# Prompt cross-attention scores: full float32 products replaced by three passes on split operands

## The chip, the core and the metric

The kernel runs on one NeuronCore of a Trainium2 chip. The metric is the device time of one execution in microseconds (us). The kernel before was timed in three runs: 813.55, 813.92 and 814.2 us, a median of 813.92 us. All times inside an execution come from one profiled execution of the same kernel.

## What is computed

The reference is one step of a decoder layer for two groups that share all weights: a prompt of 512 tokens and a sample group of 8 sequences of 4 tokens. A layer has a mixer (dilated attention and a gated recurrence), a cross-attention to a memory of 256 rows, and a feed-forward block. The change sits in the cross-attention, which reads in short:

```python
c = rmsnorm(x, norm_cross)
cq = (c @ w_cq).reshape(B, T, X_H, X_DH)                    # 4 heads of 128
s = jnp.einsum('bthd,bmhd->bhtm', cq, mem_k) * (X_DH ** -0.5)
pr = jax.nn.softmax(s, axis=-1)
co = jnp.einsum('bhtm,bmhd->bthd', pr, mem_v).reshape(B, T, X_W)
x = x + co @ w_co
```

For the prompt, mem_k and mem_v are projected from the memory inside the kernel; for the sample group they are read from a cache. All inputs and outputs are float32.

## The kernel before, in words

The activations lie transposed: 128 features on the partitions, the 512 prompt tokens and 32 sample tokens (544 columns) along the free axis. Every large projection is computed in two cuts of the columns, 0 to 255 and 256 to 543 (`CUTS`), and as three float32r passes: both operands are split into a high half (rounded to float32r, a copy on ACT) and a low half (the rest, a subtraction on DVE), and high x high, high x low and low x high are added up in PSUM. `split_half` (line 884) does such a split for an activation tile, `split_hi` and `split_lo` for a weight tile. Some small products are made with plain float32 operands instead; the prompt's scores against the memory are among them.

The memory's keys are written into two tiles `mk` (line 1707), two heads of 128 x 256 in each; the values into `mvt`, which are split into `mv_hl` (line 1863). The cross-attention then goes as follows.

- `dense_by_half` (line 856) computes cq. It runs the four heads' first cut, then calls `cq_after` (line 1896) for the four heads, then the four heads' second cut, and calls `cq_after` again. `cq_evac` scales the result out of PSUM into `cqT[h]` on DVE.
- `cross_prompt(h, part)` (line 1865) is called for each head and part. A part is 256 prompt tokens, two query blocks of 128. It makes the scores (two products of 128 x 128 by 128 x 256 into one PSUM bank, tile `ps_cp`), the row maxima (DVE, `cmx`), the exponentials (ACT, tile `cp`), the scaling by the reciprocal sum (one block on DVE, one on POOL), four transposes (`ps_cpt`), their split (`cpt..h`, `cpt..l`), the product with the split values (`ps_cpo`, three passes for each of the two blocks of memory rows), and the split of the result into `coh` and `col`. In the second part it also calls `cross_sample_scores` (line 1817), the sample group's scores (`ps_cs`), which use only 32 columns of the array at a time.
- `cross_sample` (line 1824) is the rest of the sample's cross-attention; its products with the cached values are `ps_cso`, and the values come in the tiles `st` from `in_mv`.
- `dense_by_half` (line 1914) then computes the output projection co, first cut of all eight blocks and then the second, from `coh` and `col`.

**What sets the order.** The instructions are not issued as written. The class `Tape` (line 251) records them as steps with an estimated length; `order` (line 435) plays a model of the five engines and picks the next step of each. Steps marked as main (the large projections) keep their order on PE. All other PE work is a side step: it is placed between main steps, in bursts, when enough of it has gathered, when it has waited long enough, or when its due time has come (line 573). Due times are worked out backwards from the users (`due`, line 397), and the estimated time of a main step is scaled by the sum of all PE lengths (`run`, line 421). A step may start only if the tiles that it writes are free. The working tiles of `A` and `R` (lines 668 and 671) come from one pool of 60 (`NA`, line 44); `leaves_room` (line 483) keeps a step from taking a tile that an earlier due step will want. PSUM has two banks for the main steps, five for side work (`PX`) and one for the sample group. Weights of w_cq and w_co are held in the same pool of 60 once they are split: four tiles for a column block of w_cq, two for one of w_co.

Of the kernel before, what the change touches and what calls it, by code (L numbers as in the profile page):

```python
# [10 lines left out]
F32 = mybir.dt.float32  # L11
F32R = mybir.dt.float32r
AF = mybir.ActivationFunctionType
ALU = mybir.AluOpType
# [640 lines left out]
def tile_decoder_step(ctx: ExitStack, tc: tile.TileContext, xT, memT, kwT, vw, s0, conv_in, mkT, mv, vecs, cst,  # L655
                      w_first, w_in, w_out, w_cq, w_ck, w_cv, w_co, w_gate, w_up, w_down,
                      yT, kT_out, vT_out, st_out, conv_out, mkT_out, mv_out, ss_out):
    nc = tape = Tape(tc.nc)
# [9 lines left out]
    def A(name, shape=None, dt=F32):  # L668
        return tape.tile(act, shape or [128, FW], dt, tag="a", name=name, bufs=NA)

    def R(name):
        return tape.tile(act, [128, FW], F32R, tag="a", name=name, bufs=NA)[:, :N]
# [4 lines left out]
    def PD(name):  # L677
        return tape.tile(psum, [128, 512], F32, tag="dense", name=name, bufs=2)

    def PX(name):  # L680
        return tape.tile(psum, [128, 512], F32, tag="aux", name=name, bufs=5)
# [26 lines left out]
    def C(name):  # L708
        lo, hi = CST_COLS[name]
        return cs[:, lo:hi] if hi <= mid else cs2[:, lo - mid:hi - mid]  # L710
# [173 lines left out]
    def split_half(src, name):  # L884
        n = src.shape[1]
        hi, lo = (R(f"{name}{p}")[:, :n] for p in "hl")
        nc.scalar.copy(hi, src)
        nc.vector.tensor_tensor(lo, src, hi.bitcast(F32), op=ALU.subtract)
        return hi, lo
# [71 lines left out]
    with tape.as_written():  # L961
# [42 lines left out]
        for n0, n in CUTS:  # L1004
            ps = PD(f"psr_mix_{n0}")
# [657 lines left out]
    for at, names in enumerate(MIX_ORDER):  # L1663
# [7 lines left out]
        else:  # L1671
            i = at - MIX_RAW
# [26 lines left out]
    ps = PX("psr_mem")  # L1699
# [7 lines left out]
    mk = [A(f"mk{i}", [128, 2, NMEM]) for i in range(2)]  # L1707
# [16 lines left out]
    for c in range(4):  # L1724
        ws.take()
        hi, lo = (t.rearrange("p k c -> p (k c)") for t in ws.whole[ws.i - 1][0][:2])
        for i in range(2):
            xh, xl = mems[2 * c + i]
            cols = slice(512 * i, 512 * i + 512)
            with tape.main():  # L1730
                for t in range(2):
                    tok = slice(128 * t, 128 * t + 128)
                    for j, (a, b) in enumerate(((xh, hi), (xl, hi), (xh, lo))):
                        nc.tensor.matmul(pcv[t], a[:, tok], b[:, cols], start=(c == 0 and i == 0 and j == 0),
                                         stop=(c == 3 and i == 1 and j == 2))
# [59 lines left out]
    def split_psum(h, ps, c0, c1):  # L1795
        hi, lo = (t[:, c0:c1] for t in co_hl[h])
        nc.scalar.copy(hi, ps)
        nc.vector.tensor_tensor(lo, ps, hi.bitcast(F32), op=ALU.subtract)

    def softmax_exp(ps, pt, name):  # L1800

        mx, den = small(f"cmx{name}", 2), small(f"cden{name}", 2)
        nc.vector.tensor_reduce(mx, ps.rearrange("p (a n) -> p a n", a=2), axis=AX.X, op=ALU.max, negate=True)
        for a in range(2):
            sl = slice(256 * a, 256 * a + 256)
            nc.scalar.activation(pt[:, sl], ps[:, sl], AF.Exp, bias=mx[:, a:a + 1], accum_out=den[:, a:a + 1])
        return den

    def softmax_scale(pt, den):
        nc.vector.reciprocal(den, den)  # L1810
        for a, eng in ((0, nc.vector), (1, nc.gpsimd)):
            sl = slice(256 * a, 256 * a + 256)
            eng.tensor_scalar(pt[:, sl], pt[:, sl], den[:, a:a + 1], None, op0=ALU.mult)
# [3 lines left out]
    def cross_sample_scores(h):  # L1817
        for g in range(2):
            kt = stream.take()
            for b in range(4):  # L1820
                nc.tensor.matmul(pss[32 * b:32 * b + 32, 256 * g:256 * g + 256], cqbd[:, 4 * g + b, h, :],
                                 kt[b], start=g == 0 and h == 0, stop=h == 3, skip_group_check=True)
# [38 lines left out]
            split_psum(h, pcs[:, 32 * h:32 * h + 32], SEQ, N)  # L1861

    mv_hl = [split_half(t[:, :512], f"mv{c}") for c, t in enumerate(mvt)]

    def cross_prompt(h, part):

        ps = PX(f"ps_cp{h}{part}")
        for a in range(2):
            qb = 2 * part + a
            nc.tensor.matmul(ps[:, 256 * a:256 * a + 256], cqT[h][:, 128 * qb:128 * qb + 128],  # L1870
                             mk[h // 2][:, h % 2, :], start=True, stop=True)
        if part:
            cross_sample_scores(h)
        pt = A(f"cp{h}{part}")
        den = softmax_exp(ps, pt, f"{h}{part}")
        softmax_scale(pt, den)
        pst = PX(f"ps_cpt{h}{part}")
        for c in range(2):
            for a in range(2):
                nc.tensor.transpose(pst[:, 256 * c + 128 * a:256 * c + 128 * a + 128],  # L1880
                                    pt[:, 256 * a + 128 * c:256 * a + 128 * c + 128], C("ident"))
        ptt = split_half(pst, f"cpt{h}{part}")
        po = PX(f"ps_cpo{h}{part}")
        for c in range(2):
            for i, (v, p) in enumerate(((0, 0), (0, 1), (1, 0))):
                nc.tensor.matmul(po[:, :256], mv_hl[c][v][:, 128 * h:128 * h + 128], ptt[p][:, 256 * c:256 * c + 256],
                                 start=c == 0 and i == 0, stop=c == 1 and i == 2)
        split_psum(h, po[:, :256], 256 * part, 256 * part + 256)

    cqT = [A(f"cq{h}") for h in range(XH)]  # L1890
# [5 lines left out]
    def cq_after(h, c):  # L1896
        if c:
            nc.gpsimd.tensor_copy(cqbd[:, :, h, 4 * h:4 * h + 4],
                                  cqT[h][:, SEQ:N].rearrange("p (b t) -> p b t", t=TS))
        cross_prompt(h, c)  # L1900
# [411 lines left out]
    for u, unit in enumerate(units + [None]):  # L2312
        per = next((each for halves, first, each in downs if first <= u and halves), (0, 0, 0, 0))
        q, b = unit.q if unit else {}, before.q if before else {}
# [72 lines left out]
    for m in range(KT):  # L2387
        t, hi, lo = (A(f"{n}z{m}", [128, k, 128], dt) for n, dt in (("wd", F32), ("wdh", F32R), ("wdl", F32R)))
# [89 lines left out]
```

## Time and profile before

| | |
|---|---|
| timed runs, median | 813.92 us |
| profiled execution, span from first to last instruction | 813.0 us |
| PE busy | 802.4 us, 99% of the span |
| DVE busy | 648.5 us, 80% |
| ACT busy | 445.0 us, 55% |
| POOL busy | 102.8 us, 13% |
| granted PE clock, mean | 0.998 |

The page gives no other time of the profiled execution than its span. PE stands for matmuls on TensorE, PEld for its weight loads, DVE, ACT and POOL for the vector, scalar and GpSimd engines; SPq marks the queue of SyncE, which issues most transfers. A line such as "PE ps_cp L650 x8" means eight recorded instructions that write the tile ps_cp; L650 is the recording helper of `Tape`, through which all instructions pass, so lines of code are told apart by tiles. A plain float32 matmul is recorded as two matmuls. Matmuls overlap, so the duration of one is longer than the distance to the next. In the timeline, square brackets hold the idle time of the engine before an instruction and what ended it.

### The profile page before, as it was taken

What the parts mean: (1) busy time and instruction counts of PE and PEld (TensorE: products, weight loads), DVE (VectorE), ACT (ScalarE), POOL (GpSimd) and SP (SyncE); (2) the same over time, 40 slices, a digit from 0 to 9 for tenths busy, and PEclk for the clock granted to TensorE, in tenths of its full rate; (3) what the DMA queues carried; (4) which work ended last, traced back from release to release, by engine and by line L of the source; (5) the groups of instructions that cost most, each with busy time, mean ns of one, the idle gap of its engine ahead of it and who ended that gap; (6) DMA issues with size and microseconds to landing.
All of it is one profiled execution on the core that took longest, in us unless ns stands there. A gap on an engine that the chain in (4) does not pass through costs nothing.

```text
span 813.0 us, 18994 instructions
## 1 busy us (share of the span) xinstructions
PE 802.4 (99%) x7531; PEld 755.4 (93%) x7531; DVE 648.5 (80%) x1458; ACT 445.0 (55%) x889; POOL 102.8 (13%) x186
## 2 busy tenths in 40 slices
PE   9999999999999999999999999999999999999996
PEld 9999986787889889999899999999999999999996
DVE  6996689966887897574689999997888788788854
ACT  7643365666657647454567655554554454445433
POOL 0021100010010000002201211211022012210013
PEclk9999999999999999999999999999999999999999
DMA  9449995955942454261734665655565555564503
GB/s 330 151 129 310 308 381 188 320 195 187 288 124 99 162 160 156 59 218 48 229 106 99 157 161 136 162 132 143 130 150 140 133 150 155 130 177 97 153 1 110
DMA packets 93065, 135.47 MB, mean 167 GB/s; under 512 B 6321, under 2 KB 60337, under 8 KB 92977
## 3 DMA queue, kind: packets, MB, share of 16 engines
q1 hardware_dynamic: 86208, 122.79, 46.8%
q0 software_dynamic: 5760, 10.49, 8.3%
q8 instruction: 59, 0.97, 0.5%
q10 hardware_dynamic: 1008, 0.99, 0.4%
q14 instruction: 30, 0.24, 0.1%
HBM read 126.17 MB, written 8.07 MB: 165 GB/s over the span
## 4 chain that ended last, share of the span: by engine, by line
PE 90%; DVE 5%; DMA 2%; ACT 2%; issue 1%; SPq 0%; DVEq 0%
PE ps_d L650 13%; PE ps_ag L650 7%; PE ps_au L650 7%; PE ps_wo L650 6%; PE ps_cu L650 4%; PE ps_cg L650 4%; PE ps_cq L650 3%; PE ps_dz L650 3%; PE ps_co L650 2%; PE ps_z_v L650 2%; PE ps_z_i L650 2%; PE ps_dg L650 2%; PE ps_du L650 2%; PE ps_z_Q L650 2%; PE ps_z_f L650 2%; PE ps_g L650 1%
## 5 line engine op out<-in xcount | busy, mean ns | idle before, releaser
L650 ACT CAST wh<-wr 128x1024 fp32r<-128x1024 f32 (+1 forms) x54 | 46.1, 873 | 45.3 <-PE ps_z_i L650 8.9
L650 DVE TENSOR_TENSOR wl<-wr,wh 128x1024 fp32r<-128x1024 f32 (+1 forms) x54 | 54.3, 1016 | 3.7 <-ACT wh L650 3.6
L650 DVE TENSOR_TENSOR xr<-xr,ps_d 128x256 f32<-128x256 f32 x80 | 34.6, 433 | 11.1 <-PE ps_d L650 10.2
L650 POOL COPY last<-ug 128x16 f32<-128x16 f32 (+1 forms) x44 | 22.6, 534 | 120.2 <-DVE ug L650 119.6
L650 DVE SCALAR_TENSOR_TENSOR cv<-ug,vec,cv 128x560 f32<-128x560 f32 x44 | 35.1, 798 | 2.5 <-ACT cv L650 1.9
L650 ACT ACTIVATE cv<-ug,vec 128x560 f32<-128x560 f32 x22 | 18.8, 856 | 15.5 <-DVE ug L650 15.4
L650 POOL TENSOR_TENSOR hvm<-hsm,cs 64x512 f32<-64x512 f32 x4 | 4.5, 1119 | 161.6 <-ACT hsm L650 161.6
L650 DVE TENSOR_TENSOR cv<-cv,r_ux 128x512 f32<-128x512 f32 (+1 forms) x44 | 18.7, 435 | 3.9 <-ACT cv L650 3.3
L650 ACT ACTIVATE P<-P,mx 128x128 f32<-128x128 f32 (+3 forms) x32 | 17.6, 553 | 6.7 <-DVE mx L650 6.7
L650 ACT ACTIVATE cv<-cv 128x560 f32<-128x560 f32 x22 | 14.8, 674 | 9.1 <-DVE cv L650 9.1
L624 POOL DMA_DIRECT2D S1u<-in_w_up x10 | 8.6, 863 | 87.4 <-DMA S1u<-in_w_up 27.6
L650 ACT COPY keptu<-ps_au 128x272 f32<-128x272 f32 x20 | 7.7, 386 | 21.1 <-PE ps_au L650 21.1
L650 ACT COPY keptg<-ps_ag 128x272 f32<-128x272 f32 x20 | 7.7, 385 | 21.0 <-PE ps_ag L650 20.7
L650 POOL TENSOR_SCALAR cp<-cp,cden 128x256 f32<-128x256 f32 x8 | 8.1, 1019 | 85.7 <-issue 76.2
L650 PE MATMUL ps_co<-coh,wh 128*128 128x256 f32 (+1 forms) x64 | 18.6, 291 | 0.0
L650 PE MATMUL ps_co<-coh,wl 128*128 128x256 f32 (+1 forms) x64 | 18.4, 288 | 0.0
L650 PE MATMUL ps_co<-col,wh 128*128 128x256 f32 (+1 forms) x64 | 18.4, 288 | 0.0
L650 DVE TENSOR_TENSOR xr<-xr,ps_wo 128x256 f32<-128x256 f32 (+1 forms) x16 | 6.8, 435 | 12.6 <-PE ps_wo L650 12.6
L650 DVE TENSOR_TENSOR xr<-xr,ps_dz 128x288 f32<-128x288 f32 (+1 forms) x15 | 6.6, 438 | 12.3 <-PE ps_dz L650 12.3
L650 PE MATMUL psdo<-st,dpt 128*32 128x256 f32 x224 | 16.2, 386 | 0.1
L650 ACT ACT_TABLE_LOAD x11 | 14.1, 1283 | 2.3 <-issue 2.1
L650 PE MATMUL psd<-st,qbd_win 128*32 128x224 f32 x256 | 15.4, 358 | 0.0
(3889 smaller groups left out, 3670.7 us busy)
## 6 DMA issues: line engine op xcount, KB each, us to landing
st<-in_kwT SPq DMA_DIRECT2D x32, 448.0 KB, 5.9
st<-in_vw SPq DMA_DIRECT2D x28, 512.0 KB, 5.7
wd<-in_w_down SPq DMA_DIRECT2D x32, 256.0 KB, 3.1
wr<-in_w_in SPq DMA_DIRECT2D x15, 512.0 KB, 6.6
wrg<-in_w_gate SPq DMA_DIRECT2D x10, 512.0 KB, 4.1
wru<-in_w_up SPq DMA_DIRECT2D x10, 512.0 KB, 4.5
st<-in_mkT SPq DMA_DIRECT2D x8, 512.0 KB, 6.8
wr<-in_w_out SPq DMA_DIRECT2D x8, 512.0 KB, 3.7
```

Of the source, the lines that this page charges most:

```text
L624: return tape.put(engine, lambda: call(*args, **kw), outs, ins, 0.1, 0.3, size)
L650: return tape.put(engine, lambda: call(*args, **kw), outs, ins, length, lag, size, port, words)
```

## The change

The keys of the memory are split once, right after the values: `mk_hl` holds a high and a low tile of 512 columns for each of the two `mk` tiles. In `cross_prompt`, a new tile `cqs` takes the high half of the part's 256 query columns (a copy on ACT) and the low half (a subtraction on DVE). Each of the two score products becomes three float32r products that add up in the same PSUM region: q high with mk high, q high with mk low, and q low with mk high; the product of the two low halves is left out, as in the kernel's other split products. Nothing else is edited; since the planner works from the recorded steps, the order of all instructions is made anew.

```diff
     mv_hl = [split_half(t[:, :512], f"mv{c}") for c, t in enumerate(mvt)]
+    mk_hl = [split_half(t.rearrange("p h n -> p (h n)"), f"mk{i}") for i, t in enumerate(mk)]
 
     def cross_prompt(h, part):
 
         ps = PX(f"ps_cp{h}{part}")
+        q = A(f"cqs{h}{part}", [128, 2, 256], F32R)
+        src, at = cqT[h][:, 256 * part:256 * part + 256], 256 * (h % 2)
+        nc.scalar.copy(q[:, 0, :], src)
+        nc.vector.tensor_tensor(q[:, 1, :], src, q[:, 0, :].bitcast(F32), op=ALU.subtract)
         for a in range(2):
-            qb = 2 * part + a
-            nc.tensor.matmul(ps[:, 256 * a:256 * a + 256], cqT[h][:, 128 * qb:128 * qb + 128],
-                             mk[h // 2][:, h % 2, :], start=True, stop=True)
+            for i, (n, m) in enumerate(((0, 0), (0, 1), (1, 0))):
+                nc.tensor.matmul(ps[:, 256 * a:256 * a + 256], q[:, n, 128 * a:128 * a + 128],
+                                 mk_hl[h // 2][m][:, at:at + 256], start=i == 0, stop=i == 2)
         if part:
             cross_sample_scores(h)
```

## The prediction

> **What bounds the kernel now.** I read the head of the page first (busy times and the chain by engine), then a table of stages, then the chain itself around the changed lines.
>
> ```profile
> span 813.0 us, 18994 instructions
> PE 802.4 (99%) x7531; PEld 755.4 (93%) x7531; DVE 648.5 (80%) x1458; ACT 445.0 (55%) x889; POOL 102.8 (13%) x186
> PE 90%; DVE 5%; DMA 2%; ACT 2%; issue 1%; SPq 0%; DVEq 0%
> ```
>
> PE is busy in 99% of the span, and 90% of the chain that ended last is PE work. The table of stages shows whether that also holds where the change sits (columns: stretch, length, then busy time and instruction count of PE, PEld, DVE, ACT, POOL; then the granted clock, DMA share, GB/s).
>
> ```profile
> 0.00:50.00 50.00, 48.27 (x362) 47.27 (x363) 42.67 (x84) 32.40 (x59) 3.64 (x10) 1.00 0.60 207
> 100.00:150.00 50.00, 48.53 (x768) 39.27 (x764) 46.20 (x138) 30.28 (x64) 2.11 (x3) 1.00 0.87 300
> 365.40:382.00 16.60, 16.60 (x124) 16.13 (x124) 7.40 (x18) 5.29 (x19) 4.19 (x5) 1.00 0.11 38
> 382.00:400.50 18.50, 18.50 (x166) 14.96 (x163) 10.63 (x23) 9.31 (x25) 2.01 (x4) 1.00 0.65 204
> 400.50:416.00 15.50, 15.41 (x166) 13.32 (x165) 13.13 (x33) 11.00 (x32) 4.10 (x5) 1.00 0.62 193
> 436.00:797.00 361.00, 361.00 (x2874) 360.95 (x2873) 301.59 (x609) 185.85 (x326) 65.25 (x128) 1.00 0.51 132
> ```
>
> From 365.4 to 400.5, where the prompt's scores are computed, PE is busy all the time at the full granted clock (1.00), while DVE and ACT are each busy for about half. From 436 to 797 PE never rests either, so a microsecond of PE time removed here should arrive at the end. The page gives the profiled execution only as its span, 813.0; the three timed runs have a median of 813.92, so about 0.9 us lies around the span, and I leave that as it is.
>
> **Step 1: the products.** Sixteen full float32 products (4 heads, 2 parts, 2 query blocks) go. Each is recorded as two matmuls, so the view of the tile ps_cp counts 32. In their place come 48 products of float32r operands, of the same 128 x 256 shape as the cq and cpo products. The chain gives whole groups of both kinds (start, length, what):
>
> ```profile
> L650 PE MATMUL ps_cp<-mk,cq x32: 377/379/483, 365.2 to 399.9; 128*128 128x256 f32 x32
> 362.57 2.82 PE ps_cq L650 x24
> 365.40 1.73 PE ps_cp L650 x8
> 373.03 1.73 PE ps_cp L650 x8
> 384.03 2.84 PE ps_cpo L650 x24
> 387.88 1.92 PE ps_cp L650 x8
> 397.18 1.08 PE ps_cp L650 x4
> ```
>
> The mean duration of one record (379 ns) can't be used, because matmuls overlap; the length of a group can. Eight ps_cp records, that is four products, take 1.73 us: 0.4325 us each. Twenty-four passes take 2.82 or 2.84 us: 0.118 us each, three of them 0.354. A product becomes 0.0787 us shorter, sixteen of them 1.26 us. This is the term that carries the forecast.
>
> [...]
>
> **Step 2: entering the products.** The visit at 387.88 took 0.19 us more than the 1.73 of the first two, and that at 397.18 took 1.08 for two products instead of 0.865, also 0.2 more. Both follow the sample's scores, which use 32 columns of the array. Is this price one of float32, which would go as well? A group of split passes behind narrow products elsewhere answers it:
>
> ```profile
> 57.26 1.65 PE psd L650 x32
> 58.91 1.70 PE ps_ck0k L650 x12
> 60.61 1.51 PE ps_ak0k L650 x12
> ```
>
> Twelve split passes take 1.70 us behind the narrow psd products and 1.51 otherwise, again 0.19. So the price belongs to the step from narrow to wide, and I take it as unchanged: 0. The bounds are three such visits without it (the third, at 399.17, stands below), a further gain of 0.6 us, and, if the new waits break the two pairs of visits that are now one group, two entries more, a loss of 0.4.
>
> **Step 3: the splits of mk and q.** ACT makes the high half, DVE the rest. The nearest rows are the same two operations on tiles of 128 x 256 and 128 x 512:
>
> ```profile
> L650 ACT CAST coh<-ps_cpo x8: 372/373/375, 384.8 to 415.5; 128x256 fp32r<-128x256 f32 x8
> L650 DVE TENSOR_TENSOR col<-ps_cpo,coh x8: 412/415/425, 386.0 to 416.2; 128x256 fp32r<-128x256 f32 x8
> L650 ACT CAST wh<-wr x19: 612/620/1054, 341.4 to 408.8; 128x512 fp32r<-128x512 f32 x16, 128x1024 fp32r<-128x1024 f32 x3
> L650 DVE TENSOR_TENSOR mk<-ps_ck,r_mem x4: 405/416/417, 277.8 to 291.6; 128x256 f32<-128x256 f32 x4
> L650 DVE TENSOR_TENSOR wl<-wr,wh x18: 672/683/1226, 342.4 to 410.7; 128x512 fp32r<-128x512 f32 x15, 128x1024 fp32r<-128x1024 f32 x3
> ```
>
> ACT gets 8 x 0.373 + 2 x 0.620 = 4.2 us, DVE 8 x 0.415 + 2 x 0.683 = 4.7 us. The mk part can run during the out projection, since mk is written by 292 us. The eight q splits fall between 364 and 400, where the table leaves ACT some 20 us free and DVE 17. As engine time they cost nothing; if their cover failed, what would show is their latency, the next step.
>
> **Step 4: the new waits.** Between the evacuation of cq (DVE) and the scores (PE) now stand a copy on ACT and a subtraction on DVE: 0.373 + 0.415 = 0.8 us and two handovers. PE takes its matmuls in the planned order, so behind a late split waits whatever was queued next on it, a half of cq or of co. On DVE the next evacuation of cq, which frees a PSUM bank, stands behind the subtraction, which waits for ACT. The timeline shows how close the two ends are (start, length, engine, what):
>
> ```profile
> 363.63 0.43 DVE L650 SCALAR_TENSOR_TENSOR cq<-ps_cq,r_cx 128x256 f32<-128x256 f32 x1 [1.32 <-ACT r_cx L650]
> 365.24 1.89 PE L650 MATMUL ps_cp<-mk,cq 128*128 128x256 f32 x8
> 396.22 0.46 DVE L650 SCALAR_TENSOR_TENSOR cq<-ps_cq,r_cx 128x288 f32<-128x288 f32 x1 [0.91 <-PE ps_cq L650]
> 399.17 1.13 PE L650 MATMUL ps_cp<-mk,cq 128*128 128x256 f32 x4
> 389.05 0.42 DVE L650 TENSOR_TENSOR col<-ps_cpo,coh 128x256 fp32r<-128x256 f32 x1 [1.44 <-PE ps_cp L650]
> L650 PE MATMUL ps_co<-coh,wh x12: 278/281/364, 400.5 to 405.1; 128*128 128x256 f32 x12
> 415.83 0.75 DVE L650 TENSOR_TENSOR col<-ps_cpo,coh 128x256 fp32r<-128x256 f32 x2
> 415.42 10.25 PE ps_co L650 x84
> ```
>
> Head 0 is ready at 364.06 and used at 365.24, 1.2 us later; head 3's second part at 396.68 and used at 399.17, 2.5 us later. Both hold the 0.8 us and the handovers. At the far end the last low half of co's input is written at 416.58. It is first needed when the first halves of co are through. Of their 96 passes 36 (three operand pairs of 12) run by 405.1, the other 60 head the group that starts at 415.42, at 0.118 each, hence until 422.5. So 5.9 us of cover remain at the end of this chain. I take 0; the bounds are 0 and 0.8 us on each of the four second-part visits, 3.2 us.
>
> **Step 5: tiles.** The pool of 60 working tiles matters, because the planner lets a step start only when its tile is free.
>
> ```profile
> 356.73 3.61 SPq L624 DMA_DIRECT2D st<-in_mv  x7
> 361.75 0.38 SPq L624 DMA_DIRECT2D st<-in_mv  x1
> 375.29 0.47 ACT L650 ACTIVATE cp<-ps_cp,cmx 128x256 f32<-128x256 f32 x1 [5.97 <-PE ps_cpt L650]
> 369.69 1.01 POOL L650 TENSOR_SCALAR cp<-cp,cden 128x256 f32<-128x256 f32 x1 [76.15 <-issue]
> 375.20 6.38 PE ps_cq L650 x48
> 389.80 6.38 PE ps_cq L650 x48
> 405.80 3.96 PE L650 MATMUL ps_cso<-st,cspt 128*32 128x256 f32 x64
> ```
>
> Around 377 us the code's tiles add up to 60: x 8, the split norm 16, w_cq 16, the eight half tiles of in_mv (all loaded by 362), mv 4, cq 4, mk 2, one row factor, one cp. The ACT row shows it: the second head's exponential waits 5.97 us, until the first head's transposes release a tile. The change holds mk as four tiles instead of two, and each q split takes one for a few microseconds, so about three more are wanted. What can yield without harm are the in_mv tiles, which are used only from 405.8 on. I take 0; what it costs otherwise is the third rival.
>
> The order of all instructions is planned anew from the changed costs. Where PE has no idle time that can move nothing; before 311 us the two stages with most of it lack 1.7 and 1.5 us, so I allow 0.3 us each way.
>
> Sum: 813.92 - 1.26 = 812.7, with 812.1 to 813.4 as this case's own range (below it the 0.6 us of step 2, above it the 0.4 of step 2 and 0.3 of replanning).
>
> **The rivals.**
> [...]
>
> Second, the gain is used up by waits: 0.3 us of uncovered handover at each of the four second-part visits, where PE waits for one head after another, gives back 1.2 us: 813.9. For it: on ACT and DVE other work stands ahead of the splits. Against it: the 2.5 us at the last head.
>
> Third, slower, by tiles: lacking a free tile, each of heads 1 to 3 has its softmax so late that its transposes miss one half of cq (6.38 / 2 = 3.19 us). The last low half of part 0 then moves by 9.6 us. It ended at 389.47, and cover lasts until the cq halves end at 396.18, 6.7 us later; PE idles 2.9 us and the net is 813.92 - 1.26 + 2.9 = 815.6. Four halves give 818.7. I take 816. It decides from 6.7 us of delay on. For it speaks the 5.97 us row; against it the in_mv tiles, and that a cq half frees four weight tiles.
>
> **How the numbers follow.** Forecast 0.56, first rival 0.15, second 0.16, third 0.13. A measurement of this kernel can tell about 0.2%, 1.63 us: faster means below 812.29, slower above 815.55. Faster: most of the first rival (0.13) and a quarter of the forecast (0.14), 0.27. Slower: the third rival, 0.13. The same: 0.60. The range goes from 811.7 (the first rival less 0.3 of replanning) to 815.6, which cuts most of the third rival.
>
> **What would show it.** In the profile after: 48 ps_cp matmuls, 24 of them in 2.8 us or 12 in 1.4; PE's busy time lower by 1.3; PE still at its whole length in 365 to 400; first co passes 1 us or so earlier. Wrong would be PE idle with cqs, cp or coh as releaser, a w_co or in_mv load that ends a wait of PE, or groups of ps_cp passes above 0.13 us each.

## The result, and the profile after

The changed kernel took 816.26 us (median of 22 runs, 814.94 to 818.98); the kernel before, run in turn with it, 814.61 us (22 runs, 813.55 to 816.74). The ratio is 1.0021, with a 95% interval of 1.0013 to 1.0029: the change costs 1.7 us where I forecast a gain of 1.3. The profiled execution of the changed kernel took 815.08 us, of which the span is 813.3: 1.8 us lie around the span, not the 0.9 that I had taken from a median and the span of a single execution.

The head of its page, as for before: the span, the busy times, and the chain by engine.

```profile
span 813.3 us, 19023 instructions
PE 801.5 (99%) x7547; PEld 756.0 (93%) x7547; DVE 652.4 (80%) x1468; ACT 447.4 (55%) x899; POOL 102.8 (13%) x186
PE 89%; DVE 6%; ACT 2%; DMA 1%; issue 1%; SPq 0%; DVEq 0%
```

PE has 0.9 us less to do, and yet the span is 0.3 us longer: PE stands still for 11.8 us in place of 10.6. The table of stages for the same stretches as before (three of them):

```profile
365.40:382.00 16.60, 16.60 (x146) 16.12 (x148) 6.30 (x14) 4.67 (x16) 0.61 (x2) 1.00 0.17 58
382.00:400.50 18.50, 18.50 (x175) 16.48 (x168) 14.43 (x34) 11.76 (x38) 5.89 (x7) 1.00 0.78 242
436.00:797.00 361.00, 360.07 (x2866) 359.80 (x2865) 300.77 (x607) 184.85 (x324) 65.96 (x128) 1.00 0.51 131
```

Where the scores are computed PE never rests, as before. It rests where nothing was edited: from 436 to 797 us it was busy for all 361.00 us before, now for 360.07. The chain around the scores:

```profile
371.97 6.36 PE ps_cq L650 x48
378.32 2.85 PE ps_cp L650 x24
396.40 3.05 PE ps_cp L650 x24
399.45 0.60 PE ps_co L650 x5
```

The 48 passes come as two groups of 24, in 2.85 and 3.05 us, and the first pass of co starts at 399.45 in place of 400.50. So the edited place is faster, as forecast. The whole cross-attention (first ps_cq to first ps_g) takes 74.5 us in place of 76.2. The view of PE's waits in the changed kernel (us in all, times, longest) shows where PE stands still instead:

```profile
PE ps_ag L650 <- DVE wlg L650: 0.9, 1, 0.9
PE psL L650 <- DVE mx L650: 0.9, 1, 0.9
PE psu L650 <- ACT hsm L650: 0.5, 1, 0.5
PE psr_hg L650 <- DVE mx L650: 0.3, 1, 0.3
```

None of these four is in the kernel before, which has in their place one wait of the recurrence:

```profile
PE psS L650 <- DVE z_v L650: 1.4, 1, 1.4
```

None of them is at a tile of the change. The first is in the FFN (ps_ag is a product of its gate, wlg the low half of the gate's weights), the others ahead of 311 us. All belong to work that both kernels do alike, in another order. A wait is not yet a loss: e9 below still has the three ahead of 311 us, and has the lowest ratio of all.

**Why the order differs.** On PE the two kernels' matmuls follow in the same order up to about 76 us and differ from there on, 270 us ahead of the first added instruction (the split of mk, at 344.7 us). The planner's estimate of when a main step is reached contains a factor, the sum of all PE lengths over the sum of those of the main steps (`run`, line 421). The cheaper scores lower it from 1.19231 to 1.18898. Every estimated time of a main step moves by 0.28%, the due times that follow from them move too, and every close choice between two steps can fall the other way.

### The profile page after: what moved, and what is told of

It is laid out like the page before. It is cut to its first block, busy times and chain, and to the rows that moved or that the text cites. A ratio compares the mean times of both kernels' runs of the same rounds, so it can differ in the third digit from the quotient of the medians.

```text
span 813.3 us, 19023 instructions
## 1 busy us (share of the span) xinstructions
PE 801.5 (99%) x7547; PEld 756.0 (93%) x7547; DVE 652.4 (80%) x1468; ACT 447.4 (55%) x899; POOL 102.8 (13%) x186
## 4 chain that ended last, share of the span: by engine, by line
PE 89%; DVE 6%; ACT 2%; DMA 1%; issue 1%; SPq 0%; DVEq 0%
PE ps_d L650 13%; PE ps_au L650 7%; PE ps_ag L650 7%; PE ps_wo L650 6%; PE ps_cu L650 4%; PE ps_cg L650 4%; PE ps_cq L650 3%; PE ps_co L650 3%; PE ps_dz L650 3%; PE ps_z_v L650 2%; PE ps_z_i L650 2%; PE ps_dg L650 2%; PE ps_du L650 2%; PE ps_z_Q L650 2%; PE ps_z_f L650 2%; PE ps_g L650 1%
## 5 line engine op out<-in xcount | busy, mean ns | idle before, releaser
L650 POOL COPY ug<-conv_state 128x16 f32<-128x16 f32 x22 | 13.5, 614 | 11.7 <-PE ps_co L650 6.1
```

The source lines that it names most:

```text
L650: return tape.put(engine, lambda: call(*args, **kw), outs, ins, length, lag, size, port, words)
```

## The experiments

Two theories stood at this point. **A:** the products gain what was forecast, and the new order of unchanged work costs more than that. **B:** the added splits on ACT and DVE cost it. Each experiment's ratio is to the kernel before, on the same chip; the last column counts the executions with a mean granted clock below 0.997. (The record of the granted clock stands at one half at the end of the profiled span, for the last 2.7 us in the kernel before and the last 5.1 in the changed one, which alone gives their means of 0.998 and 0.997. The five profiled runs at 0.993 to 0.996, of e2, e3, e6, e8 and e10, have a further fall; that the other executions with such means have one too is my reading.)

| kernel | products | order | median us | ratio, 95% interval | below 0.997 |
|---|---|---|---|---|---|
| before | old | old | 814.4 to 815.1 | 1 | 22 of 105 |
| changed | new | new | 816.26 | 1.0021, 1.0013 to 1.0029 | 14 of 22 |
| e1 | new | old | 813.64 | 0.9986, 0.9975 to 0.9996 | 1 of 12 |
| e2 | old | new | 819.23 | 1.0047, 1.0031 to 1.0064 | 5 of 7 |
| e3 | old, with the splits | new | 818.41 | 1.0037, 1.0021 to 1.0052 | 5 of 8 |
| e4 | old | a third | 815.17 | 0.9999, 0.9991 to 1.0008 | 0 of 11 |
| e5 | new | new, psds later | 814.67 | 1.0007, 0.9997 to 1.0017 | 0 of 11 |
| e6 | new | new, wlg earlier | 815.73 | 1.0020, 1.0009 to 1.0032 | 4 of 12 |
| e7 | new | e5 and e6 | 814.50 | 0.9997, 0.9988 to 1.0006 | 0 of 11 |
| e8 | new | old, psds earlier | 817.25 | 1.0025, 1.0012 to 1.0037 | 10 of 12 |
| e9 | new | e5, old from the FFN on | 813.76 | 0.9983, 0.9974 to 0.9992 | 0 of 11 |
| e10 | new | old, new from the FFN on | 815.34 | 1.0003, 0.9994 to 1.0013 | 6 of 12 |
| e11 | new | e7, whg earlier | 813.65 | 0.9986, 0.9977 to 0.9994 | 0 of 11 |
| e12 | new | new, bunch parted by cv | 815.29 | 1.0005, 0.9994 to 1.0017 | 1 of 11 |

### Order against products: e1 to e4

The factor is set by hand. e1 is the changed kernel, e2 and e4 are the kernel before:

```diff
-        scale = sum(s.length for s in self.steps if s.engine == "PE") / sum(s.length for s in self.mains)
+        scale = 1.1923103090901321    # e1: that of before
+        scale = 1.1889838040188532    # e2: that of the changed kernel
+        scale = 1.1956                # e4: one as far off on the other side
```

With that, e1's planned order is that of before up to the cross-attention, and e2's that of the changed kernel. e3 keeps the changed kernel's order and splits, but issues each triple of passes as one float32 product of the two high halves; it leaves out the low halves' part of the scores.

> The changed kernel, but the planner's time scale of the main steps is held at the value that it has in the kernel before (1.19231 in place of 1.18898), so that the planned order is that of before up to about 348 us, where the split of mk comes in. Theory A (the new products gain about 1.3 us and the rest is the new order of unchanged work): the out projection starts at 311.2 as before, not 311.95, so 0.7 us or more comes back: 813.3 to 815.5, ratio to before 0.998 to 1.001. If the wait of PE for wlg near 457 us belongs to the new order too, it is gone and the ratio is 0.998. Theory B (the added splits on DVE and ACT and their waits cost more than the products gain): nothing comes back, 816.3, ratio 1.002.

> The kernel before, all its instructions unchanged, with only the planner's time scale set to the value of the changed kernel (1.18898). Theory A: the order of the first 348 us is that of the changed kernel, the out projection starts near 311.95, and the time rises by 0.7 us or more: 815.3 to 817, ratio 1.001 to 1.003. Theory B: no instruction differs, so the time is that of before, ratio 1.000.

> The changed kernel with its planned order kept, but each triple of split products is issued as one full float32 product (of the high halves, so the scores lack the low halves). Only the PE price of the products differs from the changed kernel. Theory A: 16 x 0.0787 = 1.26 us more than the changed kernel, 817.5, ratio to before 1.0036. [...] Theory B (waits, not PE, set the time around the scores): as the changed kernel, 816.3, ratio 1.002.

> The kernel before with only the planner's time scale moved as far the other way (1.1956). Theory A: another order of the same work, so the time moves by some tenths of a microsecond to 2 us, either way: ratio 0.998 to 1.0025, not the same as before. Theory B: ratio 1.000.

The four corners of products and order agree with A. New products at the old order: 0.9986. Old products at the new order: 1.0047. The order costs 0.47% with the old products and 0.35% (1.0021 over 0.9986) with the new. e3 has all of the splits' load and is no slower than e2, which has none (818.41 us for 819.23): B falls. Two sizes were not as A had them: e2 lies above the 1.001 to 1.003 that I had expected, and e4 did not move at all. The size of the gain shows in the profiles of the same order: the cross-attention takes 75.8 us in e3 and 74.5 in the changed kernel, 1.3 us.

e4 shows that a changed factor isn't a loss by itself: this one shift of the same size to the other side costs nothing (0.9999). What counts is the particular order that comes out.

### The clock: e5, e8 and e12

In the profiled runs of e2 and e3 the trace's record of the granted clock falls from 1.0 to 0.5 once, for 3.413 us. The table of stages for e2, the 3.41 us ahead of the fall and then the fall (granted clock: third number from the end), with PE busy throughout:

```profile
293.25:296.66 3.41, 3.41 (x35) 2.66 (x27) 3.21 (x7) 1.54 (x6) 1.17 (x2) 1.00 0.07 24
296.66:300.07 3.41, 3.41 (x10) 2.88 (x11) 3.38 (x13) 0.18 (x1) 0.00 (x0) 0.50 0.56 173
```

The timeline shows the matmuls that it hits. First the changed kernel, in an execution without it (start, length, what), then e2 at the same place:

```profile
293.72 0.64 PE L650 MATMUL psin<-hst,z_Q 128*32 128x128 f32 x16
294.30 1.96 PE L650 MATMUL psds<-cs,domn 128*128 128x16 f32 x16
296.19 1.13 PE L650 MATMUL psu<-hvm,hsm 32*128 32x512 f32 x4
297.38 0.63 PE L650 MATMUL psin<-cs,hin 128*128 128x32 f32 x4
298.17 0.39 PE L650 MATMUL ps_cv<-wh,mml 128*128 128x512 f32 x1
298.40 0.39 PE L650 MATMUL ps_cv<-wl,mmh 128*128 128x512 f32 x1
```

```profile
293.50 1.96 PE L650 MATMUL psds<-cs,domn 128*128 128x16 f32 x16
295.39 1.13 PE L650 MATMUL psu<-hvm,hsm 32*128 32x512 f32 x4
297.98 0.63 PE L650 MATMUL ps_cv<-wh,mml 128*128 128x512 f32 x1
298.41 0.63 PE L650 MATMUL ps_cv<-wl,mmh 128*128 128x512 f32 x1
```

A cv pass follows the one ahead of it by 0.23 us in the first and by 0.43 in the second. Ahead of it both have psin, psds, psu and psin in a row, some 4 us of narrow matmuls: 32 rows or columns of the array at a time, or streams of only 16 or 32 columns. I call this run the bunch. (psds are sums of the sample group's attention, psin and psu belong to the recurrence, ps_cv is the projection of the memory's values.) In the order of before psds stands elsewhere:

```profile
301.07 1.85 PE L650 MATMUL psds<-cs,domn 128*128 128x16 f32 x16
302.77 0.48 PE L650 MATMUL psr_att<-sqh_att,blk_r 128*128 128x512 f32 x1
```

Three experiments move steps in the finished plan and leave the plan alone otherwise. A list entry names steps by number, the step that they go next to, and the side (the comments behind # are not in the kernels):

```diff
-        done = self.order()
+        done = moved(self.order())
...
+# e5, in the changed kernel: psds behind the first twelve cv passes, with its ACT and DVE steps
+MOVES = [((1349,), 1395, 1), ((1350, 1351, 1352), 1402, 1), ((1353,), 1403, 1)]
+# e8, in e1: psds, its two inputs and its ACT steps ahead, behind psU
+MOVES = [((1345,), 1347, 1), ((1348,), 1381, 1), ((1349,), 1221, 1), ((1350, 1351, 1352), 1244, 1)]
+# e12, in the changed kernel: the first six cv passes between psds and psu
+MOVES = [((1394,), 1349, 1)]
```

> The changed kernel with the 16 narrow state sums psds (and the three ScalarE steps and one VectorE step behind them) issued about 7 us later, between two cv passes, as the kernel before has them; all else in the changed kernel's order. Theory A (the new order bunches psin, psds, psu and psin into 3.7 us of tiny matmuls, after which the granted clock falls to one half for 3.41 us in part of the executions): fewer executions with a mean clock below 0.997 (the changed kernel had 14 of 22, the one before 7 of 26), and about 1 us less than the changed kernel: ratio 1.000 to 1.001 where the changed kernel had 1.0021. Rival R (the cost of the new order is spread over many small waits and the bunch has no part in it): ratio and clocks as the changed kernel, 1.0015 to 1.003.

> The mirror: the changed products in the old order (which had 0.9986, and 1 of 12 executions with a mean clock below 0.997), with the state sums psds moved 7 us earlier into the run of narrow matmuls, as the new order has them, and the two VectorE steps and three ScalarE steps that belong to them. Theory A: more than a third of the executions with a mean clock below 0.997 and 0.5 to 1.2 us more: 0.9992 to 1.0002. Rival R (the bunch does nothing by itself): 0.998 to 0.999 and clocks as before the move.

> The changed kernel with nothing altered but TensorE's order at one place: the first six cv passes (128x512, 1.4 us) go between psds and psu, in the middle of the run of narrow matmuls, and psds stays where the new order has it. Theory C (the clock falls where a stretch of about 3.4 us holds next to no wide pass, whichever matmuls make it up): the run of narrow matmuls is now in two pieces, the clocks are those of e5 (none below 0.997, or few), ratio 1.000 to 1.0012, with PE's wait for wlg left as it is. Rival D (it is psds at that place, or the number of narrow matmuls, that does it): half of the executions below 0.997 and ratio 1.0015 to 1.0025.

The clocks of all three went as theory A (C for e12) has it. Moved out of the bunch (e5), no execution of 11 is below 0.997, and the ratio falls from 1.0021 to 1.0007; the two intervals overlap, so the time alone would not settle it. Moved into it in the old order (e8), 10 of 12 are, and the ratio rises from 0.9986 to 1.0025, and these intervals do not touch: 3.2 us more, where I had expected 0.5 to 1.2. With the bunch cut in two by wide passes, and nothing else altered (e12), 1 of 11 is below, at 1.0005: by the clocks neither the place of psds nor the number of narrow matmuls decides, but an unbroken stretch of them. Why e8 costs more is in its trace: half clock for 6.827 us, twice 3.413. Its bunch also holds the whole of psU, and the second half of the bunch is itself slowed:

```profile
293.19 1.16 PE L650 MATMUL psU<-hvt,hkt 128*128 128x128 f32 x8
294.19 1.86 PE L650 MATMUL psds<-cs,domn 128*128 128x16 f32 x16
296.31 0.79 PE L650 MATMUL psin<-cs,hin 128*128 128x32 f32 x4
297.02 2.08 PE L650 MATMUL psu<-hvm,hsm 32*128 32x512 f32 x4
299.63 0.63 PE L650 MATMUL ps_cv<-wh,mml 128*128 128x512 f32 x1
300.48 0.63 PE L650 MATMUL ps_cv<-wh,mmh 128*128 128x512 f32 x1
```

psu takes 2.08 us for the 1.13 of the changed kernel.

The falls lie on a grid. Each begins a whole number of times 3.413 us after the record of full clock begins: 85 times in e2, e6 and e8 (290.13 us), 86 in e3, 37 in e10. Full clock without a fall is on record for 805.55 us in the kernel before and 802.13 in the changed one, 236 and 235 times the same 3.4133. In e2 the stretch of 3.413 us ahead of the fall (293.25 to 296.66) holds narrow matmuls only. In the changed kernel's profiled run, which has no fall here and whose record begins at 6.00 us, the same grid has a boundary at 296.13, in the middle of the bunch, so that no stretch holds it whole: the one behind the boundary has 1.7 us of cv passes in it. Where the grid lies differs between the profiled executions: the record begins 4.3 to 10.4 us into their spans. How much wide work in a stretch keeps the clock up is not settled here: e8's fall came although 1 us of psU, 128x128 products, lay in the stretch ahead of it.

How the clock comes to fall behind such a stretch, and why only some executions of the same order are hit, no run shows. That the place of the grid decides it would fit e2 and the changed kernel; with one run without a fall to compare, that stays argued. Idle time of PE was not needed: PE was busy for all of the 3.41 us ahead of e2's fall, and the clock fell all the same.

### The FFN: e6, e7, e9, e10 and e11

From the first ps_g to the first ps_dz the kernel before takes 344.1 us, the changed one 345.2. The two put PE's matmuls in the same order there. The tiles are these: whg and wlg are the high and low half of the gate's weights wrg, cv is the FFN's convolution (not the projection ps_cv), S3g2l is the low half of a sum of weights that is needed later, and keptg is a copy of a gate product. The timeline of ACT and DVE around the place where the changed kernel's PE waits, first for the kernel before, which has no wait there:

```profile
454.44 1.05 ACT L650 CAST whg<-wrg 128x1024 fp32r<-128x1024 f32 x1 [0.68 <-PE ps_u L650]
455.40 0.67 ACT L650 ACTIVATE cv<-cv 128x560 f32<-128x560 f32 x1
455.60 1.22 DVE L650 TENSOR_TENSOR wlg<-wrg,whg 128x1024 fp32r<-128x1024 f32 x1
456.74 0.69 DVE L650 TENSOR_TENSOR cv<-cv,r_ux 128x512 f32<-128x512 f32 x1
```

And for the changed kernel, which reaches this stage 1.0 us earlier:

```profile
454.15 0.68 ACT L650 ACTIVATE cv<-cv 128x560 f32<-128x560 f32 x1 [1.91 <-DVE cv L650]
454.73 1.03 ACT L650 CAST whg<-wrg 128x1024 fp32r<-128x1024 f32 x1
455.07 0.68 DVE L650 TENSOR_TENSOR cv<-cv,r_ux 128x512 f32<-128x512 f32 x1
455.67 0.69 DVE L650 TENSOR_TENSOR S3g2l<-S3g,S3g2h 128x512 fp32r<-128x512 f32 x1
456.27 1.22 DVE L650 TENSOR_TENSOR wlg<-wrg,whg 128x1024 fp32r<-128x1024 f32 x1
```

On both engines the gate's weights and cv's weighing have changed places, and on DVE S3g2l came ahead as well. So wlg, which PE needs, is ready 0.7 us later though PE is 1.0 us earlier. e6 puts wlg first on DVE; e7 is e5 and e6; e11 is e7 with whg first on ACT too.

```diff
+# e6, in the changed kernel
+MOVES = [((1951,), 1933, 0)]
+# e11: the moves of e5, and these
+MOVES += [((1950,), 1932, 0), ((1951,), 1933, 0)]
```

> The changed kernel with one VectorE step moved: the low half wlg of the gate's weights is made ahead of cv's weighing and of S3g2's low half, two places earlier in VectorE's queue. Theory A: the 0.9 to 1.1 us for which PE waits for wlg near 457 us goes and nothing takes its place: ratio about 1.001 where the changed kernel had 1.0021, and the FFN stage (first ps_g to first ps_dz) 344.1 us again in place of 345.2. Rival R: what was moved back is late next (cv's weighing holds up PE's next eviction), and the time stays: 1.002.

> Both moves together in the changed kernel. Theory A: the two costs are apart and add, so the changed kernel's products keep their gain: ratio 0.9985 to 0.9995, as the changed products in the old order had 0.9986. Rival R: 1.0015 or more.

> As e7 (state sums later, wlg two places earlier on VectorE), and ScalarE's cast whg, from which wlg is worked out, one place earlier too, ahead of cv's activation. In e6 and e7 PE still waited 0.4 to 0.5 us for wlg, because VectorE then stood 0.65 us for whg. Theory A2: PE waits for neither whg nor wlg near 456 us, FFN near 344.3 us, ratio about 0.999. Rival R3 (cv's activation, now 1 us later, holds up the next evictions and PE waits there): 0.9997 as e7 or more.

e6 was a miss. The FFN still takes 345.1 us, and PE's waits there are now two:

```profile
PE ps_ag L650 <- DVE wlg L650: 0.5, 1, 0.5
PE ps_ag L650 <- ACT keptg L650: 0.4, 1, 0.4
```

DVE then stood for whg, which ACT makes behind cv, so the wait for wlg only shrank from 0.9 to 0.5 us; and PE lost that again some 10 us later to a copy of ACT. e7 (0.9997) misses the range that I had expected and is little better than e5 (1.0007); the intervals overlap. With whg first as well (e11) the wait for wlg is gone, the FFN takes 344.6 us, and the ratio is 0.9986; this interval overlaps that of e7 too. The wait of 0.4 us for keptg is left.

e9 and e10 join the two plans at the FFN's first gate product, and so test the rest of the order as a whole:

```diff
+def spliced(tape, new):
+    t = 0.0
+    for s in tape.mains:
+        s.est = t
+        t += s.length * OLD
+    old = tape.order()
+    one, two = (new, old) if FIRST == "new" else (old, new)
+    head = one[:[s.number for s in one].index(1904)]
+    inside = {s.number for s in head}
+    return head + [s for s in two if s.number not in inside]
```

> The new order (with the state sums moved later, as in e5) up to the first gate product of the FFN, and from there the order that the planner gives under the scale of before. PE's order is that of e5 throughout; in the FFN only VectorE, ScalarE, GpSimd and the DMA queues are put otherwise. Theory A2 (what e5 leaves of the loss is the 1.1 us that the FFN stage gained, 345.2 for 344.1 us, all of it PE's wait for wlg, and the new order of stage 1 costs nothing beside the clock): FFN 344.1 us, no wait of PE for wlg, ratio 0.9985 to 0.9995 where e5 had 1.0007. Rival R2 (the rest lies in the order of the recurrence ahead of 311 us): 1.000 to 1.001.

> The other half: the old order (as in e1, which had 0.9986) up to the first gate product of the FFN, and from there the new order. Theory A2: FFN 345.2 us with PE's wait of about 1 us for wlg, clocks as in e1, ratio 0.9995 to 1.0003. Rival R2: 0.9982 to 0.999, as e1.

The stretch 436 to 780 us in the table of stages, for e9 and then for e10:

```profile
436.00:780.00 344.00, 344.00 (x2744) 344.00 (x2743) 295.39 (x594) 177.12 (x308) 59.48 (x122) 1.00 0.52 138
```

```profile
436.00:780.00 344.00, 343.07 (x2735) 342.85 (x2734) 295.46 (x595) 178.12 (x310) 60.14 (x122) 1.00 0.53 138
```

With the old FFN order PE has no gap, and e9 is at 0.9983, where e1 was (0.9986): ahead of the FFN the new order costs nothing beside the clock that these runs could tell, with intervals of 0.1% each way. With the new FFN order the 0.9 us gap is back, and e10 is at 1.0003, 0.17% above e1. Part of that may be the clock: 6 of e10's executions are below 0.997, against 1 of 12 for e1, although PE's order is the same in both and I had expected e1's clocks. The order of before has a stretch of narrow matmuls of its own, near 130 us, with idle time in it: in e10's profiled run PE was busy for 1.94 of the 3.41 us ahead of a fall, most of the rest being its wait of 1.43 us for z_v. Behind it the run shows the half clock (a ps_z_v pass of 288 columns each 0.24 us, where 0.13 is usual). The table of stages ahead of that fall, and the timeline:

```profile
129.48:132.89 3.41, 1.94 (x14) 1.41 (x13) 3.32 (x14) 1.61 (x5) 0.00 (x0) 1.00 0.76 258
```

```profile
128.52 1.05 PE L650 MATMUL psL<-kq 128*32 128x32 f32 x24
131.70 0.41 PE L650 MATMUL psS<-cs,z_v 128*32 128x128 f32 x2 [1.43 <-DVE z_v L650]
133.92 0.45 PE L650 MATMUL ps_z_v<-xm3l,wh 128*128 128x288 f32 x1
134.16 0.45 PE L650 MATMUL ps_z_v<-xm3h,wl 128*128 128x288 f32 x1
```

That the kernel before is itself hit there in 22 of 105 executions would fit; I did not alter that stretch, so it stays argued.

e9, e1 and e11 beat both kernels, the one before by 0.14 to 0.17%: the change was worth having, with its order looked after.

## Why the prediction was wrong

**Step 1, the products: right.** 1.3 us measured (e3 against the changed kernel), 1.26 forecast. A pass takes 2.85 / 24 = 0.119 us; a float32 product took as long as 3.67 passes in the trace of before (0.4325 us, at 0.118 for a pass). No run shows the larger gain that the first rival and the range's lower end of 811.7 us stand on; the runs showed 1.3 us in its place.

**Step 2, the entries: right, with a detail.** The group behind the narrow ps_cs took 3.05 us, 0.2 more than the other: the price of the entry stays. The new order enters once in place of three times. That does not explain the other 0.4 us of the 1.7 that the cross-attention gained (76.2 us before, 75.8 in e3): e2 still enters three times (8 records in 1.92 us and twice 4 in 1.06) and takes 75.8 as well. Where the 0.4 comes from stays open.

**Step 3, the splits: right.** The view of the tiles:

```profile
L650 ACT CAST cqs<-cq x8: 402/409/426, 373.4 to 392.8; 128x256 fp32r<-128x256 f32 x8
L650 DVE TENSOR_TENSOR cqs<-cq,cqs x8: 414/416/430, 375.6 to 395.3; 128x256 fp32r<-128x256 f32 x8
L650 ACT CAST mk0h<-mk x1: 616/616/616, 344.7 to 344.7; 128x512 fp32r<-128x512 f32 x1
L650 DVE TENSOR_TENSOR mk0l<-mk,mk0h x1: 684/684/684, 346.5 to 346.5; 128x512 fp32r<-128x512 f32 x1
```

Of the four, only the copy on ACT differs, 0.409 us for 0.373: ACT's 4.5 us in place of 4.2, hidden. e3, with all of them, was no slower than e2.

**Step 4 and step 5's tiles: right.** PE waits for nothing from 359 to 436 us. The three rivals did not happen: the products gained what was forecast and not more, no wait took the gain inside the stage, and no lack of tiles made PE wait. The result lies near the third rival's 816 us, and for another reason.

**The step that failed is the last of step 5**: "The order of all instructions is planned anew", with 0.3 us allowed each way. In place of 0.3 the runs show 0.35% (e1 against the changed kernel), 2.9 us. The result is 3.6 us above the forecast of 812.7; the other 0.7 is the kernel before, which took 813.92 in three runs and 814.61 in 22. The changed kernel's loss comes apart as follows, each in per cent of the time before: products -0.14 (e1); half clock +0.14 (e5 against the changed kernel; about 1.1 us); order of ACT and DVE in the FFN +0.24 (e9 against e5). They add up to +0.24 where +0.21 was measured; that is no proof of the shares, since the last two together are no more than the distance from the changed kernel to e9. The half clock has a second witness: the changed kernel's eight executions at 0.997 or 0.998 have a median of 815.4 us, 0.9 below that of all 22. The last term is the least certain: its interval is about 0.14 each way, and the traces account for 1.1 us, 0.13%, of it (345.0 us in e5, 343.9 in e9).

My reason, "Where PE has no idle time that can move nothing", fails twice. PE's missing idle time shows that the old order had enough cover, not how much. A few steps of 0.7 us each that came ahead of wlg, cv on ScalarE, cv and S3g2l on VectorE, took it all. And the span of a busy PE isn't fixed: the same narrow matmuls, put side by side, lowered its clock (e8: below 0.997 in 10 of 12 executions, e1: in 1 of 12). I had also bounded the effect by the two stages that did idle, ahead of 311 us, and the FFN, which is 344 us long and did not, lost 1.1 us.

## What to carry to other kernels

Where a planner orders the instructions, a change of one step's cost is a change of the whole order: find which of its numbers are global (here one factor), hold them fixed in a first experiment, and so part the edit from its reordering before either is judged. Idle time of zero on the bounding engine is no bound on what a new order can cost; look at how late the inputs arrive that it needs next. Look for long runs of narrow matmuls: here, with some 4 us of them in a row, the mean clock was below 0.997 in 14 of 22 executions, and with six wide passes (1.4 us) in their middle in 1 of 11.

## What was not expected of the hardware

- The granted clock of PE was halved for 3.413 us (e2, e3), or 6.827 (e8), behind a run of narrow matmuls with hardly any idle time between them; in e10 the 3.41 us ahead of the fall held a wait of 1.43 us. In the trace's record the fall and the slow matmuls lie at the same place (296.66 to 300.07 us in e2, slow cv passes from 297.4 to 300.1).
- One such stretch of half clock costs by estimate 0.8 to 1.5 us: e10's executions at a mean clock of 0.995 have a median of 816.02 us, those at 0.997 of 814.49; in the changed kernel it is 816.14 for 815.31. Two cost about 3 (e8: 817.35 at 0.993, 814.04 at 0.997, the latter from two executions only; the changed kernel: 818.07 for 815.31). By its length one such stretch lowers the mean over 813 us by 0.002 (3.413 x 0.5 / 813); how many stretches an execution without a profile holds is worked out from that.
- Whether it comes differs from one execution to the next of the same kernel on the same chip (the changed kernel: 8 of 22 at 0.993 or 0.994, 6 at 0.995, 8 at 0.997 or 0.998). A single profiled run without it, as the changed kernel's, shows nothing of this loss; the list of clocks of the timed runs does.
